# Seven half-size products for the gates of a gated linear attention layer, and a norm weight moved into a split

## The chip, the cores and the metric

The kernel runs on one core of one Trainium2 chip. The time is device microseconds from one launch of the whole program, the median of several runs: 1243.69 us over three runs (1243.62 to 1244.11). TensorE (PE in the profile) multiplies matrices, VectorE (DVE), ScalarE (ACT) and GpSimd (POOL) work on tiles in SBUF and PSUM, and SyncE (SP) issues most of the DMA transfers.

## The reference

The input x has 512 tokens of 1024 features, float32. Two layers follow one another, the first with gated linear attention (GLA), the second with gated DeltaNet (GDN); each layer ends in a gated ConvFFN. After each of the four sublayers stands `h = layer_norm(ALPHA * h + f(h))`. What bears on the change, in GLA:

```python
proj = x @ w_in                       # 512x1024 @ 1024x3088
q, k, v, gate, gk_lr = split(proj)    # 512, 512, 1024, 1024, 16 columns
gk = log_sigmoid(gk_lr @ w_gk2 + b_gk) / 16
o = rms_norm(gla_chunked(q, k, v, gk), norm_w)      # 4 heads of 256 values, norm_w has 256
return (from_head_chunks(o) * silu(gate)) @ w_out   # 512x1024 @ 1024x1024
```

GDN ends in the same way, with 8 heads of 128 values and a norm weight of 128:

```python
o = rms_norm(gdn_chunked(q, k, v, beta, g), norm_w)
return (from_head_chunks(o) * silu(gate)) @ w_out
```

## The kernel before, in words

**Products.** Every float32 operand of a large product is held as two tiles: a high part, rounded by a copy on ACT, and a low part, the difference formed on VectorE. `split_out` issues the pair; in the profile both carry its line, L579 (`wh`, `wl` for weights; `xh`, `xl` for the activations, which lie feature by token). One large product is then three matmuls, high by high, low by high, high by low, issued by `tm_terms` or `fm_mms` through `mm` (L195). A `tm` product makes 128 tokens by 512 output features in a PSUM bank, and one such bank takes 8 chunks of 128 input features x 3 matmuls of 128x512. Transposes (`tr`, L212) put four 128x128 blocks in one bank.

**Weights.** The plan (`plan_fm`, `plan_tm`, `plan_out`, `plan_fold`) lists all weight tiles of the program in order. A weight tile is 128x1024 floats, 512 KB: eight chunks of 128 outputs (fm), or two chunks of 512 outputs (tm). `prefetch` issues the load of a tile on SP's queue into one of 3 raw buffers and its split into one of 4 pairs of split buffers, some tiles ahead of their use (`LOOKAHEAD` is 2). All loads go through SP's queue in the plan's order; tiles of the kind "fold" may be loaded further ahead by `load_ahead`.

**Order of work.** The kernel is emitted by one loop over the products, with side work as generators: `spawn` puts one on a list with a due time, `pump` continues those whose time has come by an estimated clock, `until` and `wait` hold a piece of work until a named flag is set. Each engine then executes its instructions in the order of emission, which in the GLA mixer, after the query and key products, the tile scheduler may still move (`pin` is False from there on).

**The GLA mixer before.** The queries and keys of four heads are eight fm tiles, with the low-rank decay input (`lr`) behind the second. For each head, `prepare` makes the decays and five scaled forms: z (L1061), na (L1062, L1064), z (L1066), the running sum bc by a scan (L1068), differences of bc (L1073, L1080, L1085, L1086), products with q and k (L1092 to L1099). `core` makes masked scores (`sa`, masked into `sc` at L1134), the state updates (`ds`; L1154, L1156) and the output `o`. Beside it run the products for v (two halves of 512 columns, 96 matmuls each). Then `gates` makes the gate by two halves of 512 columns, four token blocks each: 96 matmuls, per block a Silu on ACT (L978) and a product with the norm's weight on VectorE (L980). `finish(hf)` waits for the four gate blocks of a half and for its two heads, multiplies output, inverse norm and gate (L1185), and calls `split_y`, which transposes four blocks per token block (yT), and splits them into `yh`, `yl` for the output product.

**The norm's weight before** is loaded once for GLA and GDN by a broadcast DMA to all 128 partitions (L683, L684), since the tokens are on the partitions where it is applied. Small vectors that are needed one value per partition go another way, `columns`: rows are loaded, and TensorE transposes them.

**A scheme that exists.** The FFN's output product (`folded`) is already made by seven products of half-size blocks instead of eight, with three pairs of accumulator banks: `FOLD` lists the seven, `issue_fold` forms the sums of weight blocks on VectorE (L355), `update` adds an accumulator to the residual when a product is done. In the profile these matmuls carry the tile name `fold`.

**Where POOL works.** POOL forms `h * g + b` of a norm's output beside the products of each layer's FFN, 16 operations of 128x512 each time (L777, L778).

Of the kernel before, what the change touches and what calls it, by code (L numbers as in the profile page):

```python
# [30 lines left out]
FOLD = [(n, FOLD_NEW[n], *FOLD_ALL[n]) for n in ("b11", "b21", "t1", "t2", "b22", "t3", "t4")]  # L31
LN_EPS = 1e-5
# [3 lines left out]
GROUPS = ((0, 8), (8, 16), (16, 22))  # L36
SLOTS = 45
# [24 lines left out]
class Trunk:  # L62
# [3 lines left out]
    def __init__(self, ctx, tc):  # L66
        self.tc = tc
        self.nc = nc = tc.nc
        self.n = 0
        ec = ctx.enter_context  # L70
        ap = ec(tc.tile_pool(name="acts", bufs=1))
        self.xh = ap.tile([P, NC, S], F32R, name="xh", tag="xh")
        self.xl = ap.tile([P, NC, S], F32R, name="xl", tag="xl")
        self.wp = ec(tc.tile_pool(name="wts", bufs=WB))
        self.hp = ec(tc.tile_pool(name="resid", bufs=2 * NTB))
        self.rp = ec(tc.tile_pool(name="raws", bufs=RAWB))
        self.cp = ec(tc.tile_pool(name="const", bufs=1))
# [4 lines left out]
        self.stage("gla", SLOTS)  # L82
# [24 lines left out]
        self.late = []  # L107
        self.parts = []
        self.after = ()
        self.first = None  # L110
        self.between = None
# [147 lines left out]

    @staticmethod  # L260
    def in_slots(item):
        return item[0] == "tm" and item[5]

    def issue(self, item):
# [4 lines left out]
        if item[0] == "fold":  # L269
            return self.issue_fold(*item[1:])  # L270
        raw = self.rp.tile([P, 1024], F32, name=self.uid("raw"), tag="raw")
# [91 lines left out]

    def prefetch(self):
# [9 lines left out]
    def load_ahead(self, until):  # L374


        self.loaded = max(self.loaded, self.issued)
        while self.loaded < min(len(self.plan), until) and self.plan[self.loaded][0] == "fold":
            _, group, _, quarter, i = self.plan[self.loaded]
            if quarter:  # L380
                self.fold_load(group, quarter, i)
            self.loaded += 1
# [248 lines left out]
    def load_x(self, x):  # L631
# [331 lines left out]
    def split_y(self, y, hf, sg):  # L963
        for tb in range(NTB):
# [3 lines left out]
            self.split_out(*t, ps)  # L968
            self.set(("y", tb, hf), 1.5)

    def gates(self, nw, width, sg):

        nc = self.nc
        r = S // width
        for hf in range(2):
            def done(tb, ps, hf=hf):
                t = self.slot("sg")
                nc.scalar.activation(t, ps, AF.Silu)  # L978
                t3 = t.rearrange("p (r d) -> p r d", r=r)
                nc.vector.tensor_mul(t3, t3, nw.unsqueeze(1).to_broadcast([P, r, width]))  # L980
# [6 lines left out]
    def gla_plan(self, w_in, w_out):  # L987
# [5 lines left out]
        for base in (1024, 2048):  # L993
            for hf in range(2):
                for cp in range(NC // 2):
                    self.plan_tm(w_in, 2 * cp * P, 2, base + hf * S)
        self.plan_out(w_out, 0, NC, TAIL)

    def gla_consts(self, w_gk2, b_gk, norm_w):
# [16 lines left out]
        self.gla_nw = self.own([P, 256], "gla_nw")  # L1016
        self.late.append((self.gla_nw, norm_w))
# [9 lines left out]
        self.spawn(self.columns([(b_gk.rearrange("(n p) -> n p", p=P), 4, self.b_gk)]), 12.0)  # L1027

    def gla(self, li, g, b):
# [146 lines left out]
        def finish(hf):  # L1176
            for tb in range(NTB):
# [3 lines left out]
            for tb in range(NTB):  # L1181
# [46 lines left out]
    def gdn_consts(self, conv_w, a_log, dt_bias, norm_w):  # L1228
# [3 lines left out]
        self.gdn_nw = self.keep([P, P], "gdn_nw")  # L1232
        self.late.append((self.gdn_nw, norm_w))
# [15 lines left out]
    def gdn(self, li, g, b):  # L1249
# [362 lines left out]
        def finish(hf):  # L1612
# [10 lines left out]
            self.split_y(y, hf, sg)  # L1623
# [13 lines left out]
        self.gates(self.gdn_nw, P, sg)  # L1637
# [79 lines left out]
```

## Time and profile before

| | |
|---|---|
| median of 3 runs | 1243.69 us |
| profiled execution | 1244.11 us, span 1242.4 us |
| granted TensorE clock | 0.998 |
| TensorE busy | 1229.4 us, 99% of the span |
| VectorE busy | 912.4 us, 73% |
| ScalarE busy | 583.2 us, 47% |
| GpSimd busy | 116.4 us, 9% |
| bytes moved | 130.73 MB, 105 GB/s on the mean |

Times in the profile are microseconds from the start of the span. In a row of the timeline stand start, length, engine, line, operation, tile out <- tiles in, the shape, and in brackets how long the engine stood idle before and what released it. "The chain" is the work that ended last, followed back from the end step by step to what released each piece.

### The profile page before, as it was taken

The numbers are of one execution on the slowest core, as the hardware profiler recorded it, in microseconds if no ns is written. First come the engines' busy times: TensorE is split into PE (matmuls) and PEld (weight loads), VectorE is DVE, ScalarE is ACT, GpSimd is POOL, SyncE is SP. The second block draws the span as 40 slices with busy tenths as digits, with TensorE's granted clock in tenths as the row PEclk, the third lists the DMA queues.
The fourth block names the chain that finished last, engine by engine and source line by source line (L and its number), as shares of the span: only waits on it lengthen the run. The fifth ranks groups of instructions, "written<-read, shape, count | busy, mean of one in ns | idle before, by whom it ended". The sixth has DMA issues, their size and how long they took to land.

```text
span 1242.4 us, 17259 instructions
## 1 busy us (share of the span) xinstructions
PE 1229.4 (99%) x6606; PEld 1039.1 (84%) x6606; DVE 912.4 (73%) x1545; ACT 583.2 (47%) x1058; POOL 116.4 (9%) x151
## 2 busy tenths in 40 slices
PE   9999999999999999999999999999999999999997
PEld 8878888988888888888988888988988888888886
DVE  4964456589966895666689966679589966796667
ACT  4644434644434443455656555543654434443440
POOL 4000000062000000001013030200044000000000
PEclk9999999999999999999999999999999999999999
DMA  7322224342353214433344341234352163223321
GB/s 208 113 75 68 68 86 136 131 141 68 99 173 102 68 51 119 119 102 104 94 145 119 85 122 46 82 123 145 111 152 85 53 202 102 85 85 102 103 67 68
DMA packets 169411, 130.73 MB, mean 105 GB/s; under 512 B 16232, under 2 KB 139946, under 8 KB 169328
## 3 DMA queue, kind: packets, MB, share of 16 engines
q1 hardware_dynamic: 164240, 120.47, 32.6%
q0 software_dynamic: 3888, 8.50, 2.2%
q8 instruction: 52, 0.85, 0.3%
q10 hardware_dynamic: 1200, 0.66, 0.2%
q14 instruction: 31, 0.25, 0.1%
HBM read 123.82 MB, written 5.78 MB: 104 GB/s over the span
## 4 chain that ended last, share of the span: by engine, by line
PE 95%; DVE 2%; ACT 1%; issue 0%; DMA 0%; SPq 0%; DVEq 0%
PE fm L195 51%; PE tm L195 23%; PE fold L195 12%; PE o L195 2%; PE xT L212 1%; PE qkT L212 1%; PE pq L195 1%; PE pg L195 1%; PE vn L195 1%; PE yT L212 1%; PE V L195 1%; DMA h<-in_x_dram 0%; PE qs L195 0%; PE ks L195 0%; PE s L195 0%
## 5 line engine op out<-in xcount | busy, mean ns | idle before, releaser
L195 PE MATMUL fm<-xh,wh 128*128 128x512 f32 (+2 forms) x1104 | 402.6, 367 | 0.7 <-ACT xh L579 0.7
L195 PE MATMUL fm<-xl,wh 128*128 128x512 f32 (+2 forms) x1104 | 400.0, 365 | 0.0
L195 PE MATMUL fm<-xh,wl 128*128 128x512 f32 (+1 forms) x1088 | 396.0, 366 | 0.0
L579 DVE TENSOR_TENSOR wl<-raw,wh 128x1024 fp32r<-128x1024 f32 (+1 forms) x162 | 202.4, 1252 | 194.2 <-ACT wh L579 192.4
L579 ACT CAST wh<-raw 128x1024 fp32r<-128x1024 f32 (+1 forms) x162 | 169.4, 1046 | 259.0 <-PE fm L195 154.4
L195 PEld LDWEIGHTS fm<-xh,wh 128*128 128x128 f32 (+1 forms) x1104 | 206.9, 188 | 33.9 <-ACT xh L579 1.1
L195 PEld LDWEIGHTS fm<-xl,wh 128*128 128x128 f32 (+1 forms) x1104 | 207.0, 188 | 32.5 <-DVE xl L579 0.2
L195 PEld LDWEIGHTS fm<-xh,wl 128*128 128x128 f32 x1088 | 204.2, 189 | 33.5
L850 DVE SCALAR_TENSOR_TENSOR conv<-fm,ffn_cw,conv 128x511 f32<-128x511 f32 x112 | 83.5, 746 | 9.7 <-ACT conv L848 8.3
L195 PE MATMUL fold<-wh,fh 128*128 128x512 f32 x224 | 87.6, 391 | 0.0
L195 PE MATMUL fold<-wl,fh 128*128 128x512 f32 x224 | 87.4, 390 | 0.0
L195 PE MATMUL fold<-wh,fl 128*128 128x512 f32 x224 | 87.2, 389 | 0.0
L195 PE MATMUL tm<-wh,xh 128*128 128x512 f32 x192 | 77.7, 405 | 1.7 <-DVE sc L1134 1.7
L579 ACT CAST wh<-b 128x1024 fp32r<-128x1024 f32 x48 | 49.6, 1053 | 60.6 <-PE fold L195 25.8
L195 PE MATMUL tm<-wl,xh 128*128 128x512 f32 x192 | 74.9, 390 | 0.0
L195 PE MATMUL tm<-wh,xl 128*128 128x512 f32 x192 | 74.8, 391 | 0.0
L868 ACT ACTIVATE conv<-conv 128x512 f32<-128x512 f32 x44 | 27.8, 632 | 80.7 <-DVE conv L850 80.7
L777 POOL TENSOR_TENSOR h<-h,gb 128x512 f32<-128x512 f32 x16 | 28.4, 1798 | 342.1 <-DMA gb<-in_ln_g_dram 342.1
L579 DVE TENSOR_TENSOR wl<-b,wh 128x1024 fp32r<-128x1024 f32 x48 | 57.9, 1219 | 2.3 <-ACT wh L579 2.3
L1244 DVE SCALAR_TENSOR_TENSOR conv<-fm,gdn_cw,conv 128x509 f32<-128x509 f32 (+2 forms) x72 | 53.4, 745 | 1.7 <-ACT conv L1242 1.1
L195 PEld LDWEIGHTS fold<-wh,fh 128*128 128x128 f32 x224 | 42.0, 188 | 9.8 <-DVE h L939 1.2
L195 PEld LDWEIGHTS fold<-wl,fh 128*128 128x128 f32 x224 | 42.0, 188 | 9.5 <-DVE wl L579 0.9
(316 smaller groups left out, 1843.4 us busy)
## 6 DMA issues: line engine op xcount, KB each, us to landing
raw<-in_ffn_w_in_dram SPq DMA_DIRECT2D x88, 512.0 KB, 3.8
raw<-in_gdn_w_in_dram SPq DMA_DIRECT2D x32, 512.0 KB, 4.1
raw<-in_ffn_w_out_dram SPq DMA_DIRECT2D x28, 512.0 KB, 3.6
b<-in_ffn_w_out_dram SPq DMA_DIRECT2D x24, 512.0 KB, 5.4
raw<-in_gla_w_in_dram SPq DMA_DIRECT2D x23, 512.0 KB, 3.6
raw<-in_gla_w_out_dram SPq DMA_DIRECT2D x8, 512.0 KB, 3.8
raw<-in_gdn_w_out_dram SPq DMA_DIRECT2D x8, 512.0 KB, 3.8
h<-in_x_dram SPq DMA_DIRECT2D x8, 256.0 KB, 6.0
```

Source lines behind the costliest of these rows:

```text
L195: t = self.nc.tensor.matmul(out, a, b, start=start, stop=stop, skip_group_check=joined)
L212: t = self.nc.tensor.transpose(out, a, self.ident[:n, :n])
L579: return self.nc.scalar.copy(dst_h, src), self.nc.vector.tensor_sub(dst_l, src, dst_h)
L777: nc.gpsimd.tensor_mul(h[hf], h[hf], gb[hf])
L850: nc.vector.scalar_tensor_tensor(a[:, d:], ps[:, :S - d], tap(2 - d), a[:, d:], ALU.mult, ALU.add)
L868: nc.scalar.activation(a, a, AF.Gelu)
L1244: self.conv = nc.vector.scalar_tensor_tensor(a[:, d:], ps[:, :S - d], tap(3 - d), a[:, d:], ALU.mult, ALU.add)
```

## The change

**Gates.** The 512x1024 by 1024x1024 product of the GLA gates is cut in 2 x 2 x 2 half blocks: tokens (256 + 256), input features (the even and the odd chunks of 128), output features (512 + 512). Seven products of half blocks (`GATED`) give the four output blocks; each is 4 chunks x 2 token blocks x 3 matmuls = 24 matmuls of 128x512, 168 in all instead of 192. The weight operands are four blocks as they are (or reused) and sums or differences of blocks; `issue_gated` forms these on VectorE (lines 396, 399, 401 of the new file; 128x1024, eight times) before the split. 14 tiles of 512 KB are loaded instead of 8. The block b11 stays in two buffers of its own (`gw`), since four of the seven need it, and is loaded by `load_ahead` as "fold" tiles are.

**Token forms.** Four of the seven products take sums or differences of token blocks (w1, v2, v4, v3). `x_forms`, spawned beside the heads, forms them on POOL: 16 operations of 128x512 (lines 1036 and 1049 of the new file), and splits them (eight casts, eight differences of 128x512).

**Two accumulators.** `gated` keeps two pairs of PSUM banks: one takes b11, t2, t3, t4 in turn, the other b21, t1, b22. `update` copies a partial sum out (ACT), adds or subtracts it (VectorE, lines 1099, 1106, 1109), and calls Silu where a block is complete; an accumulator continues to sum where the scheme lets it.

**Norm weight.** It is no longer multiplied into the gate. After the transposes the feature is on the partition, so `split_y` applies it there: ACT copies with a scale per partition (line 1020), VectorE forms `yT * w - yh` in one operation (line 1021). For GLA a tile has two heads' halves and is done in two pieces; for GDN in one. The weight comes through `columns`; the copies and broadcast loads of L683 and L684 go. `finish` in GLA becomes four tasks, one for each half of the columns and half of the tokens.

GLA's slot memory grows by two slots (`GLA_SLOTS`). The diff, cut to its core:

```diff
+GATED = (("b11", "a11", 0), ("b21", "a12", 1), ("t1", "w1", 1), ("t2", "v2", 0), ("b22", "v4", 1), ("t3", "v3", 0),
+         ("t4", "a22", 0))
+GATED_NEW = {"b11": "b11", "b21": "b21", "t1": "b12", "t2": "b22", "b22": "b22", "t3": "b11", "t4": "b21"}
...
+GLA_SLOTS = 47
...
+    def plan_gated(self, w, col):
+        group = {"w": w, "col": col}
+        for name, _, _ in GATED:
+            for i in (0, 2):
+                self.plan.append(("gated", group, name, i))
...
+    def gated_load(self, group, name, i):
+        if name == "b11":
+            t = self.mp.tile([P, 1024], F32, name=self.uid("gw"), tag="gw", bufs=2)
+        else:
+            t = self.rp.tile([P, 1024], F32, name=self.uid("raw"), tag="raw")
+        quarter = GATED_NEW[name]
+        col = group["col"] + (2 - int(quarter[2])) * S
+        c0 = 2 * i + int(quarter[1]) - 1
+        src = group["w"].rearrange("(c p) f -> p c f", p=P)[:, c0:c0 + 3:2, col:col + S]
+        self.nc.sync.dma_start(t.rearrange("p (j f) -> p j f", j=2), src)
+        group[name, i] = t
+    def issue_gated(self, group, name, i):
+        nc = self.nc
+        t = group.pop((name, i))
+        if name == "b11":
+            group["sum", i] = t
+        total = group["sum", i]
+        if name in ("t1", "t2"):
+            nc.vector.tensor_add(total, total, t)
+            t = total
+        elif name == "t3":
+            nc.vector.tensor_sub(t, total, t)
+        elif name == "t4":
+            nc.vector.tensor_add(t, total, t)
+            del group["sum", i]
+        self.vec(1.24)
+        self.held += 1
+        wh = self.wp.tile([P, 1024], F32R, name=self.uid("wh"), tag="wh")
+        wl = self.wp.tile([P, 1024], F32R, name=self.uid("wl"), tag="wl")
+        self.split_out(wh, wl, t)
+        self.vec(1.24)
+        return [(wh[:, blk(j, S)], wl[:, blk(j, S)]) for j in range(2)]
...
-            for t, row in self.late:
-                nc.gpsimd.tensor_copy(t[:, :1], self.xl[:, NC - 1, S - 1:].bitcast(F32))
-                nc.gpsimd.dma_start(t, row.partition_broadcast(P))
...
-    def split_y(self, y, hf, sg):
-        for tb in range(NTB):
+    def split_y(self, y, hf, sg, nw, blocks=range(NTB)):
+        nc = self.nc
+        for tb in blocks:
             ps = self.psum("yT")
             self.tr4(ps, sg[tb][hf])
             y[tb][hf] = t = self.slot("yh", F32R), self.slot("yl", F32R)
-            self.split_out(*t, ps)
+            n = nw.shape[1]
+            view = lambda a, i: a.rearrange("p (c n i) -> p n c i", n=n, i=P)[:, i]
+            for i in range(n):
+                yh, yl, src = (view(a, i) for a in (*t, ps))
+                nc.scalar.mul(yh, src, nw[:, i:i + 1])
+                nc.vector.scalar_tensor_tensor(yl, src, nw[:, i:i + 1], yh, ALU.mult, ALU.subtract)
             self.set(("y", tb, hf), 1.5)
-    def gates(self, nw, width, sg):
-
-        nc = self.nc
-        r = S // width
+    def x_forms(self, forms):
+        nc = self.nc
+        pair = lambda t: t.rearrange("p (j i) -> p j i", j=2)
+        def part(x, odd, tok, k):
+            return x[:, 4 * k + odd:4 * k + odd + 3:2, tok:tok + 256]
+        def full(odd, tok):
+            ts = [self.slot("xq") for _ in range(2)]
+            for k, t in enumerate(ts):
+                nc.gpsimd.tensor_add(pair(t), *(part(x, odd, tok, k) for x in (self.xh, self.xl)))
+            return ts
+        def split(name, ts):
+            forms[name] = []
+            for t in ts:
+                h, l = self.slot("xfh", F32R), self.slot("xfl", F32R)
+                self.split_out(h, l, t)
+                forms[name].append((h, l))
+            self.set(("form", name), 2.0)
+        def both(a, b, op, out):
+            for x, y, o in zip(a, b, out):
+                nc.gpsimd.tensor_tensor(o, x, y, op)
+        a, b = full(0, 256), full(1, 256)
+        both(a, b, ALU.subtract, b)
+        yield 14.0
+        split("w1", b)
+        c = full(0, 0)
+        both(c, a, ALU.subtract, a)
+        yield 10.0
+        both(b, c, ALU.subtract, b)
+        yield 5.0
+        split("v2", b)
+        c = full(1, 0)
+        both(b, c, ALU.add, b)
+        yield 10.0
+        split("v4", b)
+        b = c = None
+        yield 3.0
+        split("v3", a)
+    def gated(self, sg, forms):
+        nc = self.nc
+        acc = [[self.psum("fold") for _ in range(2)] for _ in range(2)]
+        top, high, right = ([None, None] for _ in range(3))
+        def operand(form, c, r):
+            if form in forms:
+                cols = slice(c % 2 * 256 + r * P, c % 2 * 256 + r * P + P)
+                return tuple(t[:, cols] for t in forms[form][c // 2])
+            chunk = 2 * c + (form != "a11")
+            tok = r * P + (256 if form == "a22" else 0)
+            return self.xh[:, chunk, tok:tok + P], self.xl[:, chunk, tok:tok + P]
+        def copied(ps):
+            t = self.slot("sg")
+            nc.scalar.copy(t, ps)
+            return t
+        def done(tb, hf, t, src):
+            nc.scalar.activation(t, src, AF.Silu)
+            sg[tb][hf] = t
+            self.set(("sg", tb, hf), 1.2)
+        def update(name, r):
+            p, x = acc[0][r], acc[1][r]
+            if name == "b11":
+                top[r] = copied(p)
+            elif name == "b21":
+                nc.vector.tensor_add(top[r], top[r], x)
+                done(r, 1, top[r], top[r])
+            elif name == "t1":
+                high[r] = copied(x)
+            elif name == "t2":
+                right[r] = copied(p)
+            elif name == "b22":
+                nc.vector.tensor_sub(right[r], x, right[r])
+                done(r, 0, right[r], right[r])
+            elif name == "t3":
+                nc.vector.tensor_sub(high[r], high[r], p)
+                done(2 + r, 0, high[r], high[r])
+            elif name == "t4":
+                done(2 + r, 1, self.slot("sg"), p)
+        self.look = 3
+        for name, form, at in GATED:
+            if form[0] in "vw":
+                self.wait(("form", form))
+            for i in (0, 2):
+                w = self.weight()
+                for r in range(2):
+                    ps = acc[at][r]
+                    for j in range(2):
+                        begin = name in ("b11", "b21", "t1") and i + j == 0
+                        self.tm_terms(ps, *operand(form, i + j, r), *w[j], begin, i + j == 3, True)
+                    if i:
+                        update(name, r)
+                    self.pump()
+                self.spend()
+            forms.pop(form, None)
+        self.look = LOOKAHEAD
+    def gates(self, sg):
...
-                t3 = t.rearrange("p (r d) -> p r d", r=r)
-                nc.vector.tensor_mul(t3, t3, nw.unsqueeze(1).to_broadcast([P, r, width]))
+                self.nc.scalar.activation(t, ps, AF.Silu)
...
-        for base in (1024, 2048):
-            for hf in range(2):
-                for cp in range(NC // 2):
-                    self.plan_tm(w_in, 2 * cp * P, 2, base + hf * S)
+        for hf in range(2):
+            for cp in range(NC // 2):
+                self.plan_tm(w_in, 2 * cp * P, 2, 1024 + hf * S)
+        self.plan_gated(w_in, 2048)
...
-        def finish(hf):
-            for tb in range(NTB):
+        def finish(hf, half):
+            blocks = range(2 * half, 2 * half + 2)
+            for tb in blocks:
                 yield from self.until(("sg", tb, hf))
             for hd in (2 * hf, 2 * hf + 1):
                 yield from self.until(("core", hd))
-            for tb in range(NTB):
+            for tb in blocks:
                 t = sg[tb][hf]
                 for hd in (2 * hf, 2 * hf + 1):
                     w = blk(hd % 2, 256)
                     nc.vector.scalar_tensor_tensor(t[:, w], o[hd][tb // 2][:, blk(tb % 2, 256)],
                                                    rr[:, hd, tb:tb + 1], t[:, w], ALU.mult, ALU.mult)
-            yield 2.4
-            self.split_y(y, hf, sg)
+            yield 1.6
+            self.split_y(y, hf, sg, self.gla_nw, blocks)
         for hd in range(GH):
             self.spawn(core(hd))
+        forms = {}
+        self.spawn(self.x_forms(forms), 2.0)
         for hf in range(2):
             def v_done(tb, ps, hf=hf):
                 v[tb][hf] = t = self.slot("v")
...
             self.x_tm(v_done)
         for hf in range(2):
-            self.spawn(finish(hf))
-        self.gates(self.gla_nw, 256, sg)
+            for half in range(2):
+                self.spawn(finish(hf, half))
+        self.gated(sg, forms)
```

More of the change, by code (lines that the diff above doesn't have):

```diff
@@ L81, in __init__ @@
         self.mp = None
-        self.stage("gla", SLOTS)
+        self.stage("gla", GLA_SLOTS)
         self.resets()
@@ L106, in __init__ @@
         self.next_block = 0.0
-        self.late = []
         self.parts = []
@@ L270, in issue @@
             return self.issue_fold(*item[1:])
+        if item[0] == "gated":
+            return self.issue_gated(*item[1:])
         raw = self.rp.tile([P, 1024], F32, name=self.uid("raw"), tag="raw")
@@ L377, in load_ahead @@
         self.loaded = max(self.loaded, self.issued)
[L378 to L381, printed above, removed]
+        while self.loaded < min(len(self.plan), until) and self.plan[self.loaded][0] in ("fold", "gated"):
+            if self.plan[self.loaded][0] == "gated":
+                self.gated_load(*self.plan[self.loaded][1:])
+            else:
+                _, group, _, quarter, i = self.plan[self.loaded]
+                if quarter:
+                    self.fold_load(group, quarter, i)
             self.loaded += 1
@@ L1015, in gla_consts @@
         self.spawn(factor(), 3.0)
-        self.gla_nw = self.own([P, 256], "gla_nw")
-        self.late.append((self.gla_nw, norm_w))
+        self.gla_nw = self.own([P, 2], "gla_nw")
         mk = self.slot("maskf")
@@ L1026, in gla_consts @@
         self.b_gk = self.own([P, 4], "gla_b")
-        self.spawn(self.columns([(b_gk.rearrange("(n p) -> n p", p=P), 4, self.b_gk)]), 12.0)
+        rows = lambda t: t.rearrange("(n p) -> n p", p=P)
+        self.spawn(self.columns([(rows(b_gk), 4, self.b_gk), (rows(norm_w), 2, self.gla_nw)]), 12.0)
     def gla(self, li, g, b):
@@ L1231, in gdn_consts @@
         self.specs.append((conv_w.rearrange("k (b p) -> (k b) p", p=P), 96, self.gdn_cw))
-        self.gdn_nw = self.keep([P, P], "gdn_nw")
-        self.late.append((self.gdn_nw, norm_w))
+        self.gdn_nw = self.keep([P, 1], "gdn_nw")
+        self.specs.append((norm_w.unsqueeze(0), 1, self.gdn_nw))
         self.gdn_al = self.keep([P, 2], "gdn_al")
@@ L1636, in gdn @@
             self.spawn(finish(hf))
-        self.gates(self.gdn_nw, P, sg)
+        self.gates(sg)
         self.wait(("r2", 1))
```

3 lines of the change are left out of this document (1 added, 2 removed).

## The prediction

> **What bounds the kernel now.** I read the engines' busy time first, then the chain of waits, then the timeline at the places where the chain leaves TensorE. The page of the profile:
>
> ```profile
> span 1242.4 us, 17259 instructions
> ...
> PE 1229.4 (99%) x6606; PEld 1039.1 (84%) x6606; DVE 912.4 (73%) x1545; ACT 583.2 (47%) x1058; POOL 116.4 (9%) x151
> ...
> PE 95%; DVE 2%; ACT 1%; issue 0%; DMA 0%; SPq 0%; DVEq 0%
> ```
>
> TensorE is busy 99% of the span, so a matmul taken away is worth its whole time, and a wait put anywhere on TensorE costs its whole time. The profiled execution took 1244.11 us, 1.7 us of them outside the span; it is the highest of the three runs, 0.42 us above their median of 1243.69. I add terms to the execution and take the 0.42 off at the end.
>
> The chain of waits (start, length, what), around the GLA mixer:
>
> ```profile
> 28.02 6.29 PE fm L195 x46
> 34.58 0.70 ACT z L1061
> ...
> 48.06 1.24 DVE bc L1068
> ...
> 67.50 1.23 DVE bc L1068
> 68.76 0.73 DVE sc L1134
> 70.69 16.15 PE tm L195 x70
> ...
> 137.73 21.80 PE tm L195 x96
> 159.53 1.75 PE yT L212 x16
> 161.28 21.81 PE tm L195 x96
> ```
>
> Two things are to be seen. From 137.73 on, where the gates are made, TensorE alone is the chain: 21.81 us / 96 = 0.2272 us for a product of 128x512. But from 34.58 to 70.69 the chain runs through VectorE, which makes the decay forms of the four heads. The busy time by stretches, and TensorE's timeline at the end of that stage:
>
> ```profile
> 48.00:55.00 7.00, 7.00 (x32) 5.77 (x32) 6.67 (x14) 4.96 (x9) 0.00 (x0) 1.00 0.26 77
> 55.00:71.00 16.00, 14.32 (x124) 11.47 (x123) 15.51 (x25) 8.82 (x15) 0.00 (x0) 1.00 0.22 67
> ```
>
> ```profile
> 67.62 0.47 PE L195 MATMUL tm<-wh,xh 128*128 128x512 f32 x1 [0.70 <-DVE sc L1134]
> ...
> 70.69 0.47 PE L195 MATMUL tm<-wh,xh 128*128 128x512 f32 x1 [0.98 <-DVE sc L1134]
> ```
>
> The columns after the length are PE, PEld, DVE, ACT and POOL, each with its count, then clock, DMA share and GB/s. VectorE is busy 22.18 of 23 us, and TensorE already stands twice for it (0.70 and 0.98 us). What delays VectorE there reaches TensorE in full.
>
> **The change, part by part.**
>
> *The products.* The gates go from 192 to 168 products: 24 x 0.2272 = -5.45 us. The scheme is in the kernel already, in the FFN's output product:
>
> ```profile
> 314.81 19.27 PE fold L195 x85
> 334.08 13.71 PE fold L195 x59
> 348.25 5.65 PE fold L195 x24
> 353.89 86.59 PE fm L195 x382
> ```
>
> There 168 products take 353.89 - 314.81 = 39.08 us against 168 x 0.2272 = 38.17, so 0.91 is lost, half of it in the hole before the last 24, where VectorE updates an accumulator. Here there are two accumulators instead of three. At each reuse (t1 after b21, t3 after b22, t4 after t3) TensorE waits for an ACT copy or a VectorE add of one tile. I walked the changed program's VectorE order through these points with the durations below: t1 waits about 0.6 (an add at L1099 queued behind a weight split), t3 and t4 about 0.5 together, and the transposes that now stand between 0.1. That is 1.2 us lost, between 0.9 (the FFN's) and 4 (rival 2). Gates: -5.45 + 1.2 = **-4.3 us**, from -4.6 to -1.5.
>
> *VectorE and the loads beside it.*
>
> ```profile
> L579 DVE TENSOR_TENSOR wl<-raw,wh 128x1024 fp32r<-128x1024 f32 x21 | 25.7, 1225 | 41.9 <-ACT wh L579 41.9
> ...
> L1185 DVE SCALAR_TENSOR_TENSOR sg<-o,gla_rr,sg 128x256 f32<-128x256 f32 x16 | 6.9, 479 | 0.1
> ...
> L980 DVE TENSOR_TENSOR sg<-sg,gla_nw 128x512 f32<-128x512 f32 x8 | 5.4, 687 | 0.7 <-ACT sg L978 0.7
> ```
>
> ```profile
> 110.00:137.73 27.73, 27.73 (x125) 23.34 (x124) 9.48 (x24) 11.63 (x24) 0.00 (x0) 1.00 0.19 58
> 137.73:185.00 47.27, 47.27 (x226) 39.56 (x226) 25.14 (x50) 18.04 (x29) 0.00 (x0) 1.00 0.27 89
> ```
>
> Fourteen weight tiles take the place of eight: 6 more splits x 1.225 = 7.4, 8 sums and differences of weights of the same size = 9.8, six updates of 0.687 = 4.1, and up to 8 splits of token forms x 0.687 = 5.5; the norm's 8 products go (-5.5). VectorE goes from 34.6 us of these 75 to about 56 of 71, 79%: TensorE covers it on the average, and costs arise only where a product waits for the one operation just queued. Bytes: 14 x 512 KB in 38 us is 193 GB/s, under the 288 GB/s that a row below shows moved.
>
> *The norm's weight in the split.* GLA: the 8 products of L980 go, and ACT's scaled copy and VectorE's fused operation (L1020, L1021) do the split by halves, 16 + 16 small ones; they lie beside the other products, and the transposes' last group moves past the end of the gates (8 of 16 left there instead of 16), which TensorE does anyway. GDN: 8 products go, the rest keeps its count. Its chain:
>
> ```profile
> 808.77 8.20 PE tm L195 x36
> 816.97 1.75 PE yT L212 x16
> 818.72 21.78 PE tm L195 x96
> ```
>
> There is no hole to close, so this is worth 0; it could cost 0.3 if the scaled copy comes late, and gains nothing. The two broadcast loads that go, and the few small transposes that come, are off the path: 0.
>
> *The early weights (start).* In the changed program SP issues the two 512 KB loads of b11 ahead of the second query/key weight, to keep them until the gates. Before:
>
> ```profile
> 10.37 7.09 SPq L279 DMA_DIRECT2D raw<-in_gla_w_in_dram  x4
> ...
> 14.76 1.05 ACT L579 CAST wh<-raw 128x1024 fp32r<-128x1024 f32 x1 [1.11 <-DMA raw<-in_gla_w_in_dram]
> ...
> 15.84 1.23 DVE L579 TENSOR_TENSOR wl<-raw,wh 128x1024 fp32r<-128x1024 f32 x1 [1.60 <-ACT wh L579]
> ...
> 19.24 8.62 PE fm L195 x72
> ...
> 8.00:16.00 8.00, 7.33 (x57) 6.83 (x58) 4.98 (x8) 4.17 (x6) 3.57 (x8) 1.00 1.05 288
> ```
>
> The DMA engines are full there (share 1.05). One MB more at 288 GB/s is 3.6 us; some of it overlaps the wait for an issue, so I take 3.2. The weight that lands at 14.76 lands at 17.9, ACT and VectorE have split it at 17.9 + 1.05 + 1.23 = 20.2, and TensorE, which turns to it at 19.24 and needs the low half for its third product (19.24 + 2 x 0.2272 = 19.7), waits 0.5 and then some tenths for the tile after it: **+0.8 us**, from 0 (the load is early enough) to 2 (the next weights are late too).
>
> *POOL's token forms.* Sixteen sums and differences of 128x512 (L1036, L1049) go to POOL, which so far has nothing to do there. In the changed program's order the first six run at about 21 to 31 us, where VectorE is not the bound. The next four wait for VectorE's z and bc of the second head, which end by 49.3 us above, so they run at about 48 to 55 us: beside the VectorE work that TensorE waits for at 67.62. The other six come at 87 to 108, with VectorE at half load. What POOL does to VectorE is shown in the FFN, where POOL forms the norm's output:
>
> ```profile
> 247.52 0.69 DVE L879 TENSOR_TENSOR form<-form,conv 128x512 f32<-128x512 f32 x1
> ...
> 254.34 0.42 DVE L888 TENSOR_TENSOR form<-form 128x256 f32<-128x256 f32 x1
> ...
> 275.56 1.47 DVE L879 TENSOR_TENSOR form<-form,conv 128x512 f32<-128x512 f32 x1
> 277.06 1.40 DVE L888 TENSOR_TENSOR form<-form 128x256 f32<-128x256 f32 x1
> ```
>
> ```profile
> 279.57 2.91 POOL L777 TENSOR_TENSOR h<-h,gb 128x512 f32<-128x512 f32 x2
> ```
>
> With POOL idle the 128x256 operation takes 0.42, beside POOL 1.40: 0.98 us more for each, and 0.78 for the 128x512. Four POOL operations among VectorE's back-to-back operations with two inputs: 4 x 0.98 = **+3.9 us**, all of it on TensorE. The ends: 0, if POOL's operations fall beside what they don't disturb, and 5. The six at 87 to 108 could hold one state update (0.48 in their own rows) by 1 us; TensorE has other products there, 0 to 1, I take 0.
>
> [...]
>
> **The sum.** -4.3 + 0.8 + 3.9 = +0.4 on 1244.11 gives 1244.5 for an execution like the profiled one, and 1244.1 against the median: no change that can be measured (0.2%, 2.5 us, is about what a measurement here can tell).
>
> **The rivals.**
>
> 1. *POOL does not hold VectorE in the head stage* (faster). For it: the rows above are of plain two-input operations, while half of the head stage's time is scans, fused and predicated operations, which may not wait. Against it: in the seven us after 49.3 most are plain ones. Then only the start and the gates count: 1243.7 + 0.8 - 4.3 = 1240.2, 0.28% faster.
>
> 2. *The gates wait for their weights* (slower). Place: t3 and t4, whose tiles come through the three raw buffers, and must be added to a kept sum before ACT may split them. A buffer's round is load, sum, cast, difference:
>
> ```profile
> raw<-in_gla_w_in_dram SPq DMA_DIRECT2D x23, 512.0 KB, 3.6
> ```
>
> 3.6 + 1.22 + 1.05 + 1.22 = 7.1 us, a third of it 2.4 per tile, against 12 x 0.2272 = 2.73 of products. Once VectorE's queue (finishing heads, splitting outputs) adds more than 1 us to a round, TensorE waits for each tile, and the last four tiles at 1 us each take the saving: 1244.1 + 4 = 1248. For it: VectorE's 79%. Against it: the pairs hold two to three tiles ahead.
>
> [...]
>
> **Chances.** Forecast 0.40 (own range 1241.5 to 1246); rival 1 0.24; rival 2 0.20; rival 3 0.16. So faster 0.24, same 0.40, slower 0.36. The range reaches from rival 1 with the FFN's smaller loss (1239.7) to rival 2 with the startup at its end (1249).
>
> **What would show it.** Right: in the changed profile a wait of TensorE for a low half near 20 us; plain VectorE operations of 1.4 to 1.7 us near 50 us, and the head stage's last wait at 75 instead of 70.69; the gates' 168 products within 39.5 us; GDN's stretch without holes as before. Wrong: VectorE at its old durations near 50 us with POOL's operations beside it; holes of more than 1 us in front of t2 to t4 with the release from wl or from the raw load.

## The result, and the profile after

The changed kernel takes 1251.79 us (median of six runs, 1251.38 to 1253.39), the kernel before 1244.11 us on the same chip (six runs): a ratio of 1.0064, 95% interval 1.0053 to 1.0076. It is slower by 7.7 us, where no change was forecast, and above the top of the range. The profiled execution took 1251.48 us, with a span of 1249.7.

The page of the changed kernel: busy times and the granted clock in 40 slices.

```profile
span 1249.7 us, 17294 instructions
...
PE 1233.7 (99%) x6584; PEld 1037.3 (83%) x6584; DVE 938.2 (75%) x1567; ACT 600.0 (48%) x1086; POOL 140.5 (11%) x165
...
PEclk9989999999999999999999999999999999999999
```

TensorE has 22 matmuls fewer in the trace and is busy 4.3 us longer. One slice of the clock is below full. The chain of waits of the changed kernel (start, length, what; lines have moved, `mm` is L198 here):

```profile
10.40 8.06 DMA raw<-in_gla_w_in_dram
18.48 1.06 ACT wh L629
...
20.84 9.58 PE fm L198 x78
...
36.27 0.70 ACT z L1218
...
73.08 21.47 PE tm L198 x84
...
100.30 1.29 PE ds L198 x6
...
132.99 1.29 PE ds L198 x6
...
227.94 2.15 PE fm L198 x18
...
444.32 33.59 PE fold L198 x144
```

The rows of before that answer to them, as far as the prediction does not show them:

```profile
65.70 0.73 DVE sc L1134
...
93.65 1.29 PE ds L195 x6
...
126.32 1.29 PE ds L195 x6
...
224.75 2.15 PE fm L195 x18
...
440.48 32.64 PE fold L195 x144
```

Between these marks the 7.3 us of the spans come and go:

| stretch | before | after | change |
|---|---|---|---|
| start to the first head's z | 34.58 | 36.27 | +1.69 |
| z to the first state product (ds) | 59.07 | 64.03 | +4.96 |
| to the third head's ds | 32.67 | 32.69 | +0.02 |
| to the first product of the FFN: gates, output product | 98.43 | 94.95 | -3.48 |
| the rest of the program | 1017.65 | 1021.76 | +4.11 |

The last row is the surprise: nothing that the program does there was changed but the norm's weight in GDN. The last rows of the two fences show it: 144 fold products of an FFN take 33.59 us instead of 32.64, with no hole; that is 0.2333 us each instead of 0.2267.

In the second stretch stands what the prediction feared. VectorE and POOL of the changed kernel, from the timeline:

```profile
51.02 1.60 DVE L1230 TENSOR_TENSOR e<-bc 128x512 f32<-128x512 f32 x1
52.55 1.78 DVE L1237 TENSOR_TENSOR e<-bc 128x512 f32<-128x512 f32 x1
54.25 1.51 DVE L1242 TENSOR_TENSOR e<-bc 128x256 f32<-128x256 f32 x1
55.69 1.51 DVE L1243 TENSOR_TENSOR e<-bc 128x256 f32<-128x256 f32 x1
57.12 0.68 DVE L1249 TENSOR_TENSOR e<-e,qk 128x512 f32<-128x512 f32 x1
```

```profile
49.81 3.97 POOL L1036 TENSOR_TENSOR xq<-xh,xl 128x512 f32<-128x512 f32 x2 [14.04 <-DVE z L1223]
53.74 3.17 POOL L1049 TENSOR_TENSOR xq<-xq,xq 128x512 f32<-128x512 f32 x2
```

Before, the first and the third of these:

```profile
49.32 0.69 DVE L1073 TENSOR_TENSOR e<-bc 128x512 f32<-128x512 f32 x1
...
50.53 0.42 DVE L1085 TENSOR_TENSOR e<-bc 128x256 f32<-128x256 f32 x1
```

Four VectorE operations take 1.5 to 1.8 us, and the next is at its old 0.68 as soon as POOL has ended. But there is more: the time of TensorE in the 3.41 us before 70.88 and in the 6.83 us behind it (columns as in the prediction; the clock is the third number from the end):

```profile
67.47:70.88 3.41, 0.80 (x14) 0.49 (x13) 3.15 (x8) 3.41 (x6) 0.00 (x0) 1.00 0.17 65
...
70.88:77.71 6.83, 5.87 (x29) 4.75 (x27) 6.64 (x10) 2.89 (x6) 0.00 (x0) 0.50 0.00 0
```

TensorE, waiting for the late heads, was busy 0.80 of 3.41 us, and then its clock is halved for 6.83 us. So there are four candidates for the loss: the early loads, POOL's hold on VectorE, the clock, and something that slows products far from the change.

### The profile page after: what moved, and what is told of

It reads as the page before. It is cut to its first block, busy times and chain, and to the rows that moved or that the text cites. A ratio compares the mean times of both kernels' runs of the same rounds, so it can differ in the third digit from the quotient of the medians.

```text
span 1249.7 us, 17294 instructions
## 1 busy us (share of the span) xinstructions
PE 1233.7 (99%) x6584; PEld 1037.3 (83%) x6584; DVE 938.2 (75%) x1567; ACT 600.0 (48%) x1086; POOL 140.5 (11%) x165
## 4 chain that ended last, share of the span: by engine, by line
PE 94%; DVE 3%; DMA 1%; ACT 1%; issue 0%; SPq 0%; DVEq 0%
PE fm L198 50%; PE tm L198 20%; PE fold L198 16%; PE o L198 2%; PE xT L215 1%; DMA raw<-in_gla_w_in_dram 1%; PE yT L215 1%; PE qkT L215 1%; PE pq L198 1%; PE pg L198 1%; PE vn L198 1%; PE V L198 1%; DVE wl L629 0%; DMA h<-in_x_dram 0%; PE qs L198 0%
## 5 line engine op out<-in xcount | busy, mean ns | idle before, releaser
L198 PE MATMUL fm<-xh,wh 128*128 128x512 f32 (+2 forms) x1104 | 402.6, 367 | 1.0 <-ACT xh L629 0.7
L198 PE MATMUL fm<-xl,wh 128*128 128x512 f32 (+2 forms) x1104 | 400.1, 365 | 0.0
L198 PE MATMUL fm<-xh,wl 128*128 128x512 f32 (+1 forms) x1088 | 396.2, 366 | 0.8 <-DVE wl L629 0.8
L198 PEld LDWEIGHTS fm<-xh,wh 128*128 128x128 f32 (+1 forms) x1104 | 206.9, 188 | 34.7 <-ACT xh L629 1.1
L198 PEld LDWEIGHTS fm<-xl,wh 128*128 128x128 f32 (+1 forms) x1104 | 207.0, 188 | 32.7 <-DVE xl L629 0.2
L198 PEld LDWEIGHTS fm<-xh,wl 128*128 128x128 f32 x1088 | 204.3, 189 | 34.2 <-DVE wl L629 1.0
L198 PE MATMUL fold<-wh,fh 128*128 128x512 f32 x224 | 88.8, 396 | 0.0
L198 PE MATMUL fold<-wh,fl 128*128 128x512 f32 x224 | 88.6, 396 | 0.0
L198 PE MATMUL fold<-wl,fh 128*128 128x512 f32 x224 | 88.6, 395 | 0.0
L198 PE MATMUL tm<-wh,xh 128*128 128x512 f32 x128 | 53.0, 414 | 1.0 <-DVE sc L1291 1.0
L198 PEld LDWEIGHTS fold<-wh,fh 128*128 128x128 f32 x224 | 42.1, 188 | 10.8 <-DVE h L985 0.9
L198 PE MATMUL tm<-wl,xh 128*128 128x512 f32 x128 | 50.9, 398 | 0.0
L198 PEld LDWEIGHTS fold<-wh,fl 128*128 128x128 f32 x224 | 42.1, 188 | 10.2
L198 PE MATMUL tm<-wh,xl 128*128 128x512 f32 x128 | 50.4, 395 | 0.0
```

The costliest lines, as they stand in the source:

```text
L198: t = self.nc.tensor.matmul(out, a, b, start=start, stop=stop, skip_group_check=joined)
```

## The experiments

In the allocation of the two programs one thing differs for the whole program: the two norm-weight tiles shrank (`gdn_nw` from 128 values per partition to 1, `gla_nw` from 256 to 2), and the tiles of a stage that lie behind them start at another place, in GLA 64 bytes past a multiple of 128, in the FFNs and GDN 32 bytes past one. Before, these tiles started at a multiple of 128. (The kernel before holds a hint of it: an unused tile `pad` of 96 bytes, line 690, without which they would not.) The first experiment gives the old addresses back:

```diff
-        self.gla_nw = self.own([P, 2], "gla_nw")
+        self.gla_nw = self.own([P, 256], "gla_nw")[:, :2]
...
-        self.gdn_nw = self.keep([P, 1], "gdn_nw")
+        self.gdn_nw = self.keep([P, P], "gdn_nw")[:, :1]
```

> The changed kernel, with the two small norm-weight tiles given their old size (only the first columns are used), so that every tile behind them in SBUF has its old start address modulo 128 bytes. Theory (the products of the FFN's folds, of the output projections and of the summed token forms take 0.2333 us each instead of 0.2270, because their token tiles start 32 or 64 bytes off): all 128x512 spacings at 0.227 again, about 1000 products x 6.3 ns = 5 to 6.5 us less than the changed kernel, 1245.3 to 1246.8. Rival (the spacing follows the clock drop at 71 us, or something else in the order of work): spacings stay at 0.2333 and the time at 1251.8.

Measured: 1247.75 us (seven runs, 1245.99 to 1248.83), 4.0 us less than the changed kernel. The clock drop is still there (a granted clock of 0.996 in the profiled execution), and the products are back at 0.227 us each; its chain:

```profile
132.95 1.29 PE ds L198 x6
...
227.21 2.15 PE fm L198 x18
...
442.86 32.64 PE fold L198 x144
```

From 227.21 to the end of its span, 1244.9, are 1017.69 us: the last row of the table is back at its old size. The theory holds for the cause. Its size was put too high, at 5 to 6.5 us: it is 4.8 between the two traced executions and 4.0 between the medians.

The same from the other side: the kernel before, with nothing changed but one tile's size.

```diff
-        self.gdn_nw = self.keep([P, P], "gdn_nw")
+        self.gdn_nw = self.keep([P, P + 8], "gdn_nw")[:, :P]
```

> The kernel before, with one persistent tile 32 bytes longer, so that every stage's tiles start 32 bytes later; nothing else. Theory (a product is slow where its moving operand, in the weight buffers at 0 modulo 128, and its stationary operand, in the stage's tiles, start at different places modulo 128): 672 fold products and 256 of the output projections at 0.2333 instead of 0.2270, 5 us more, 1248 to 1250; products with both operands in the stage's tiles keep 0.227. Rival (addresses don't matter by themselves): 1244.1.

> The kernel before, the same tile 64 bytes longer, so that the stage's tiles start 64 bytes later. Theory (any start that differs modulo 128 counts, as the GLA tiles of the changed kernel at 64 suggest): the same 0.2333 and 1248 to 1250. Rival (only 32 counts, 64 is a boundary of its own): 0.227 and 1244.1, and then GLA's slow products in the changed kernel had another cause.

Measured: 1248.64 and 1248.54 us (P + 8 and P + 16) against 1244.14, ratio 1.0039 (1.0024 to 1.0054) for 32 bytes: 4.4 to 4.5 us for 32 or for 64 unused bytes. The chain of the 32-byte and of the 64-byte version:

```profile
441.87 33.59 PE fold L195 x144
```

```profile
441.47 33.60 PE fold L195 x144
```

Which address counts? A matmul has two operands: the stationary one is loaded by an instruction of its own (LDWEIGHTS of 128x128, 0.19 us each, PEld in the profile: 6606 of them before, one for each of the 6606 matmuls), the other is the moving one. In the folds of these two versions the moving operand (the split weights, in the weight buffers) stays at 0 and the stationary one (the FFN's forms, in the stage) moves. The last experiment moves both by 32 bytes, and leaves only xh and xl at 0:

```diff
+        skew = ap.tile([P, 8], F32, name="skew", tag="skew")
+        nc.gpsimd.memset(skew, 0.0)
         self.wp = ec(tc.tile_pool(name="wts", bufs=WB))
```

> The kernel before, with 32 unused bytes behind the activations: the weight buffers and the stage's tiles both start 32 bytes later, only the activations xh, xl stay at 0 modulo 128. Theory A (the difference between the two operands' starts counts): fold and yh products with the weight buffers back at 0.227, though both operands are at 32, and all products of xh, xl with the weight buffers at 0.2333, some 3000 x 6.3 ns = 19 us more, 1260 to 1265. Theory B (the start of the stationary operand counts): fm (stationary weight at 32) and fold (stationary form at 32) slow, tm from xh (stationary at 0) fast, 1264 to 1268. Theory C (the start of the moving operand counts): tm and fold slow, fm fast, 1249 to 1252.

Measured: 1260.30 us, ratio 1.0131 (1.0114 to 1.0148). Its chain:

```profile
138.72 22.39 PE tm L197 x96
...
357.12 89.13 PE fm L197 x382
446.25 32.67 PE fold L197 x144
```

The folds, with both operands at 32, are fast again (32.67). The fm products (moving xh at 0, stationary weight at 32) are slow: 89.13 / 382 = 0.2333 against 86.59 / 382 = 0.2267 before. The tm products (moving weight at 32, stationary xh at 0) are slow too: 22.39 / 96 = 0.2332. With both operands at 0 a fold product takes 32.64 / 144 = 0.2267, with both at 32 it takes 0.2269, with 32 between them 0.2333: it is the difference of the two starts modulo 128 that counted in these runs, as theory A has it; B or C, with one operand alone, would have left tm or fm fast, and the folds slow. The differences tried (32 and 64 bytes in the stationary operand, 32 in the moving one) cost nearly the same, 6.1 to 6.7 ns a product of 128x512. Products of 128x256 show nothing of it: the 720 fm products of that shape have a mean busy time of 281 to 284 ns in this run and 283 to 286 before, where those of 128x512 go from 389 to 391 up to 395 to 398.

Now the head stage. POOL's second group of sums waits for the last head's forms instead:

```diff
             for k, t in enumerate(ts):
+                if late is not None:
+                    nc.gpsimd.tensor_copy(t[:, :1], late[:, :1])
...
-        c = full(0, 0)
+        yield from self.until(("prep", 3))
+        c = full(0, 0, prep[3][2])
```

> The changed kernel, with the second group of four POOL sums made to wait for the last head's forms (about 76 us), so that none runs beside the head stage. [...] Rival (VectorE is slow there for another reason, or the clock drops because of the late start): no more than 1 us less, 1250.8 to 1251.8.

Measured: 1247.09 us (ten runs), 4.7 less than the changed kernel, where the rival allowed 1. No half clock is left behind its head stage (from 72.28 on its products start 0.23 us apart), and its first state product is 1.89 us behind that of before, instead of 6.65:

```profile
72.28 17.51 PE tm L198 x76
...
95.54 1.29 PE ds L198 x6
```

The same cause put into the kernel before, where nothing else is new: sums on POOL that nobody reads, behind the second head's scan.

```diff
             nc.vector.tensor_tensor_scan(bc, self.reset, z, 0.0, ALU.mult, ALU.add)
+            if hd == 1:
+                t, u = self.own([P, S], "spare0"), self.own([P, S], "spare1")
+                nc.gpsimd.tensor_copy(t[:, :1], bc[:, :1])
+                nc.gpsimd.tensor_copy(u[:, :1], bc[:, :1])
+                for w, x in zip((t, u), (0, 2)):
+                    nc.gpsimd.tensor_add(w, self.xh[:, x], self.xl[:, x])
+                nc.gpsimd.tensor_add(t, t, u)
+                nc.gpsimd.tensor_add(u, t, u)
```

(Lock, in this expectation and in that on the early loads, is a name for the hold that the traces show: 1.51 to 1.78 us for VectorE operations that take 0.42 to 0.69 with POOL idle.)

> The kernel before, with four POOL sums of 128x512 whose results nobody reads, started behind the second head's scan at 49.3 us; nothing else is changed. Theory (lock): four of VectorE's two-input operations behind the scan at 1.5 to 1.8 us instead of 0.42 to 0.69, head stage 4 us later, TensorE's wait at 67.6 about 4.5 us long, perhaps with a half clock after it: 1247.5 to 1249.5. Rival (the lock is covered by something in the head stage): 1244.1 to 1245.

> The kernel before, with two POOL sums behind the second head's scan instead of four. Theory A (the half clock comes only after a wait of TensorE that is long enough): VectorE 2 us later, TensorE's wait some 2 us longer than before, clock at full speed throughout: 1246 to 1246.5, so half the sums cost less than half of the 4.4 us. Theory B (any longer wait brings the half clock): full clock lost for 6.8 us again, 1247 to 1247.6.

Measured: four sums 1248.52 (ratio 1.0038, 1.0023 to 1.0053), two sums, without the last two lines, 1245.97 (1.0017, 1.0008 to 1.0026). The two ran on different chips, and each ratio is to the kernel before on its own chip (1244.14 and 1243.79). VectorE of the version with four, the stretch before its clock drop, its first mask of the late heads (`sc`) and its first state product:

```profile
49.96 0.42 DVE L1093 TENSOR_TENSOR e<-bc 128x256 f32<-128x256 f32 x1
50.30 1.51 DVE L1094 TENSOR_TENSOR e<-bc 128x256 f32<-128x256 f32 x1
```

```profile
65.95:69.36 3.41, 1.20 (x24) 1.07 (x24) 3.12 (x8) 3.38 (x6) 0.00 (x0) 1.00 0.02 8
```

```profile
69.07 0.72 DVE sc L1142
...
98.20 1.29 PE ds L195 x6
```

And the same two of the version with two:

```profile
67.55 0.73 DVE sc L1140
...
95.50 1.29 PE ds L195 x6
```

Two neighbours of the same shape, one at 0.42 and one at 1.51 us: POOL had started in between, at 50.05. With four sums the state product comes 4.55 us later than in the kernel before, and the clock is halved for 6.8 us; with two it comes 1.85 us later at full clock. At the mask, VectorE is late by 1.85 us with two sums and by 3.37 with four (65.70 before). With two, the state product is late by no more than that; with four, by 1.18 more, and that is the half clock. So of the two theories A agrees with the traces. The times alone would not show it: 2.2 us for two sums and 4.4 for four, where theory A had said less than half. And the version with two may be near the edge: one of its ten executions took 1247.17 us, 1.2 more than their median, at a granted clock of 0.996, which is that of the version with four.

The early loads: pinned to their place in the program's order.

```diff
-        self.nc.sync.dma_start(t.rearrange("p (j f) -> p j f", j=2), src)
+        load = self.nc.sync.dma_start(t.rearrange("p (j f) -> p j f", j=2), src)
+        if name == "b11":
+            self.tc.keep_in_program_order(load)
```

> The changed kernel, with the two loads of b11 held in the program's order behind the loads for v. Theory (the 1 MB in front of the second query/key weight costs 1.6 us at the start, one to one): first wide product after the split at 19.2 us instead of 20.8, time 1.6 us less, 1250.2, if the two loads are not late at the gates. Rival (the loss is taken up by the waits of the head stage, which end later for the lock): 1251.8.

Measured: 1250.05 us, 1.7 less, as expected. The 80 products that began at 20.84 begin earlier by 2.1 us:

```profile
18.73 9.56 PE fm L198 x80
```

All three edits together:

> The changed kernel with the three edits together: old addresses, POOL's second group late, b11's loads late. Theory (these are all the losses): what stays is the gates' 24 products less and some tenths of holes, -5.45 + 0.6 to 1.2, so 1239.3 to 1240 against 1244.1 before. Rival (the three overlap or the gates themselves lose more): 1242 to 1245.

Measured: 1240.62 us (ten runs), ratio 0.9974 (0.9964 to 0.9983) to the kernel before: 0.26% faster, and 11.2 us less than the change as made (the three alone: 4.0 + 4.7 + 1.7 = 10.4). It is 0.6 above the theory's range and below the rival's, that the gates lose more themselves or the three overlap:

```profile
94.11 1.29 PE ds L198 x6
...
126.78 1.29 PE ds L198 x6
...
165.27 1.52 PE yT L215 x8
...
221.00 2.15 PE fm L198 x18
```

From 126.78 to 221.00 are 94.22 us, 4.21 less than before. The version that beats both kernels is the change with two padded tiles, the loads of b11 pinned and one group of sums later.

What is the part with the norm's weight worth? Alone, in the kernel before, with the tiles padded:

> The kernel before with the norm-weight part alone (weights per partition in the split, the products with the gate and the broadcast loads gone), its small tiles at their old sizes so that addresses stay; the gates are made as before. Theory (these products lie beside TensorE's): 1243.6 to 1244.6. Rival (the scaled split comes late at the gates' end, or the products that go were on the path): more than 1 us either way.

Measured: 1244.95 us, ratio 1.0007 (0.9998 to 1.0017): no difference that can be measured. And taken out of the version with all three edits, that is, with the broadcast loads and the products with the gate put back:

```diff
             nc.scalar.activation(t, src, AF.Silu)
+            self.weigh(t, self.gla_nw, 256)
...
-                nc.scalar.mul(yh, src, nw[:, i:i + 1])
-                nc.vector.scalar_tensor_tensor(yl, src, nw[:, i:i + 1], yh, ALU.mult, ALU.subtract)
+            self.split_out(*t, ps)
```

> The version of the fourth experiment without the norm-weight part: gates by seven products, old addresses, POOL's second group late, b11's loads late, but the norm's weight loaded broadcast and multiplied into the gates on VectorE as before (8 products more in GLA's gate stage). Theory (the norm-weight part is beside TensorE's work in both mixers): the same as the fourth experiment within 0.8 us, 1239.8 to 1241.4. Rival (with VectorE busier in the gates, the norm's products would now delay the updates of the accumulators): 1 to 2 us more, 1241.6 to 1242.6.

Measured: 1245.47 us (ten runs), ratio 1.0011 (1.0002 to 1.0021), 4.85 more than with that part: more than either theory gave. (The two ran on different chips; each set against the kernel before on its own, it is 5.2.) Its chain:

```profile
31.54 4.65 DMA raw<-in_gla_w_in_dram
...
97.15 1.29 PE ds L199 x6
...
129.82 1.29 PE ds L199 x6
...
225.04 2.15 PE fm L199 x18
```

From 129.82 to 225.04, the marks of the gates, are 95.22 us, 1.0 more than in the version with all three edits: that is the rival, VectorE too busy in the gates. The greater part, 3.0 us, is lost before the first state product (97.15 against 94.11), and it begins at 26 us; VectorE and POOL there, and the clock at the end of the head stage:

```profile
25.96 5.56 DVE L632 TENSOR_TENSOR wl<-raw,wh 128x1024 fp32r<-128x1024 f32 x1 [4.53 <-ACT wh L632]
```

```profile
22.91 5.03 POOL L1040 TENSOR_TENSOR xq<-xh,xl 128x512 f32<-128x512 f32 x4
27.91 2.52 POOL L1053 TENSOR_TENSOR xq<-xq,xq 128x512 f32<-128x512 f32 x2
```

```profile
70.73:74.14 3.41, 3.33 (x8) 2.69 (x9) 3.32 (x5) 0.87 (x2) 0.00 (x0) 0.50 0.00 0
```

The broadcast loads go out on POOL ahead of its first group of sums, which begins 2.6 us later for it (20.34 in the version with all three edits) and holds a weight split for 5.56 us, where that version's took 2.07 and an undisturbed one takes 1.23. Its raw buffer comes free late, and the load that needs it goes out at 31.54 and lands at 36.19; and behind the waits at the end of the head stage the clock is halved again, for 3.41 us. So the norm part is worth nothing by itself, and some 1 us beside seven products. The 3 us look like an accident of place that comes from POOL again; that is read from this trace, and no run tests it.

## Why the prediction was wrong

The sum put two things at nothing that were not: the sizes of the norm's small tiles, at 0 without a look at where the later tiles would start (4.0 us between the medians, 4.8 between the traces), and the half clock of TensorE behind its long wait (1.2 us). The early loads were put 0.9 too low. POOL's hold on VectorE and the gates, the terms that the prediction worked on most, came out at their size. By its own steps:

- **What bounds the kernel.** Right: VectorE is the chain from 34 to 71 us, and its delay reached TensorE. TensorE's first late product moved from 67.62 to 73.08, 5.46 us; 1.69 of it is the start, which leaves 3.77 to POOL's hold on VectorE.
- **The products, -4.3 us.** Right in size: -4.21 with all three edits, -4.17 with the addresses alone mended (132.95 to 227.21). The change as made shows -3.48, since the 0.7 between went to slow products of the summed forms and the output. The parts of the 1.2 us lost were not as walked, so that the sum came out right is in part luck: in the version with all three edits TensorE's products are 0.2 us late at t1 and 0.2 at t4, instead of 0.6 and 0.5, and eight transposes take 1.52 us instead of 0.87 (the row at 165.27), since they wait for the output's product with the gate on VectorE. The bound taken from the FFN was misread too; its hole before the last 24 products is none, since two fm products of another weight stand there, and 0.5 was lost and not 0.9:

```profile
347.80 0.45 PE fm L195 x2
```

- **The early weights, +0.8 us.** Right in mechanism, mis-sized: the row at 18.48 instead of 14.76 is 3.7 us late, not 3.2, and TensorE waited for the high half as well; 1.69, inside the bound of 2.
- **POOL's token forms, +3.9 us.** The mechanism was right and the size too: 0.91 + 1.10 + 1.09 + 1.09 = 4.19 for the four. The first six sums, which the step costed at nothing, cost TensorE nothing where they fell, but seem to have done so in the version without the norm part, where a weight split was held for 5.56 us. That split was held for longer than one POOL operation, which took 1.26 us there (5.03 / 4). The traces show that VectorE operations take longer beside POOL's, and by how much; they do not show what holds them.
- **"All of it on TensorE" left out what the wait itself does.** The state product was 6.65 us late, not 5.46. The half clock from 70.88 to 77.71 takes more than the 1.19 between, by my estimate 2.17 us, since a wait of 0.98 that TensorE had before is gone behind it. The half-clock stretches in the traces are 6.83 us here, twice 3.41, about 6.8 with four unread sums, and 3.41 without the norm part. In the 3.41 us before the drop TensorE was not idle: it worked 0.80 us of them here, 1.20 with four unread sums and 1.29 without the norm part. The trace of before had no such stretch between its first and its last product (its clock is 1.00 up to 1236 us), and no rival had this loss.
- **"GDN: worth 0", and the small tiles at 0.** Here the prediction failed by most. The operations were costed, and the run with that part alone bears out their 0; the sizes of the tiles that held the weight were not looked at. They moved the tiles of every stage, and the stretch behind GLA lost 4.1 us, which with the 0.7 in GLA is 4.8 of the 7.0 between the sum's 1244.5 and the profiled execution's 1251.48.

With these in place the prediction's own sum comes out: 1244.5, + 0.9 at the start, - 0.1 for POOL's hold, + 1.2 for the clock, + 4.8 for the addresses, + 0.1 for the gates is 1251.4, against 1251.48 for the profiled execution. The terms are read from the same two traces, so that they add up is no proof; the test of a term is the run that takes it out. The start and the addresses have one each; POOL's hold and the clock are taken out only together. The lower end of the range is 1239.9 by its own terms, not 1239.7; nothing hangs on it.

Of the rivals, the first is refuted by the four rows at 51 to 57 us and by the two experiments with unread sums. The second did not occur: the gates with mended addresses are at the forecast. The third, with the start and POOL's hold at the upper ends of their ranges (2 and 5 us), had the right two terms, at 1.7 and 3.8, but not the two that made the case.

What stays open: when a wait of TensorE brings the half clock. It came behind 3.41 us with 0.80, 1.20 and 1.29 us of work (the last without the norm part); the trace with two sums has 3.41 us with 1.22 of work (66.06 to 69.47, counted from the rows of its timeline) and no half clock behind them, so the amount of work alone does not tell. Why the operands' relative start costs 6.1 to 6.7 ns stays open, and differences other than these were not tried. Nor is it known why a weight split lost 0.8 us beside POOL's first sums in one version and 4.3 in another.

## What to carry to other kernels

Before a small persistent tile is resized, look at where every later tile then starts: on this chip 32 bytes cost 4.5 us in 1244 without one instruction changed, and padding takes it back. Work given to an idle POOL was free here only where VectorE was not the chain (the four sums beside the head stage cost 4.7 us); its time must be chosen by a dependency and not left to when its inputs happen to be ready. A wait added to a TensorE that waited already cost its clock on top, 1.2 us with four unread sums and nothing with two, so two short waits may be cheaper than one long one; that last step is my inference, and no run tests it.

## What the runs showed of the hardware that was not expected

- A 128x512 fp32r product took 0.2267 to 0.2271 us where the moving and the stationary operand started at the same place modulo 128 bytes (both at 0, or both at 32), and 0.2332 to 0.2333 where they differed by 32 (whichever of the two was moved) or 64. Products of 128x256 did not get slower: a mean busy time of 281 to 284 ns with a difference of 32, and 283 to 286 before.
- A 128x1024 VectorE operation that met POOL's back-to-back sums took 5.56 us instead of 1.23 in the version without the norm part, until about 1.1 us behind the last sum, while four of 128x512 and 128x256 in the changed kernel lost 0.91 to 1.10 us each.
- The tensor clock was halved for 6.83 us in the changed kernel, for about 6.8 with four unread sums and for 3.41 in the version without the norm part, each time behind 3.41 us in which TensorE was at work for 0.80, 1.20 and 1.29 us.
